# Forgetting attention: the second copy of k is taken from the first one in SBUF, and the last pair of heads is shaped one head later

## The chip, the core and the metric

One core of a Trainium2 chip runs the whole layer as one program. The metric is the device time of one execution in microseconds (us). The kernel before takes 1297.82 us, the median of three executions (1297.64 to 1299.04).

TensorE (PE) multiplies matrices and transposes; ScalarE (ACT) and VectorE (DVE) scale, copy and reduce; GpSimd (POOL) and SyncE (SP) mostly issue DMA transfers. TensorE writes its results to eight PSUM banks, everything else lies in SBUF.

## The reference, cut to what matters

The layer is a feed-forward block, a mixing block, and a second feed-forward block over 512 tokens of width 1024, in fp32. The mixing block has an mLSTM branch (4 heads) and a forgetting attention (16 heads of width 64); gates join the branches. The change touches the forgetting attention:

```python
q = jnp.moveaxis(rms_norm(q, q_g), 1, 2)
k = jnp.moveaxis(rms_norm(k, k_g), 1, 2)
logits = jnp.einsum('bhqd,bhkd->bhqk', q_blk, k).astype(f32) * scale + (F_blk[..., :, None] - F[..., None, :])
logits = jnp.where(k_pos[None, :] <= q_pos[:, None], logits, -jnp.inf)
p = jax.nn.softmax(logits, axis=-1)
return jnp.einsum('bhqk,bhkd->bhqd', p.astype(v.dtype), v)
```

## The kernel before, in words

**Two-part numbers.** To keep fp32 accuracy, an operand x is split into a rounded high part (type fp32r) and a low part, x minus high. A product takes three matmuls, high by high, high by low, low by high (`mm3`, L145 to L147). ScalarE makes the high part (`split`, L120) and VectorE the low part (L122) of every weight tile.

**The attention stage.** Heads go in pairs: pair p holds heads 2p and 2p+1, and two pairs make a group g. `fox_qkv` (L1354) multiplies the group's q and k; for groups 1 to 3 they are written to HBM (L1386) and come back turned, 16 small transfers into four tiles `fT` (`bring`, `blocks`, L1350). These lie in the tag `tok`, which has 4 buffers. For group 0, TensorE turns them into a PSUM bank instead (L1449).

`fox_t(p)` (L1428) brings a pair into shape: from the source `b` (a PSUM bank for pairs 0 and 1, an `fT` tile in SBUF for the others) it makes for each of the two heads a q tile with the high part in one half of the partitions and the low part in the other, a k tile with the high part in both halves, and a tile `klz` with k's low part in one half and zeros in the other. ScalarE writes the high parts (L1453) and k's second copy (L1455); VectorE writes the low parts (L1459). Two matmuls per block of queries then give all three products. In `fox_t`, ScalarE has 6 instructions for a pair and VectorE 4, each over 64 partitions and 512 columns; no transfer is issued.

The loop in `run` (from L1833) goes over n, the head: `fox_s(n)` gives scores and exponentials (L1483 and L1484 on TensorE, L1486 and L1490 on VectorE, L1494 on ScalarE), `fox_o(n-2)` multiplies by v (L1543, L1546, L1547), then perhaps `fox_t`, then `fox_p(n-1)` scales the rows (L1507 on ScalarE from head 9 on), transposes them into three PSUM banks (L1513) and splits these (L1511 on ScalarE, L1512 on VectorE). The scores and these transposes take turns in the four banks of the pool `pt`. Between these calls `advance(fill, ...)` steps through work that keeps TensorE busy: projections of the next group and gates (L1591), and from n = 12 on the output gate of the mLSTM branch, `y_a(m)`: it loads the weights of m+1 (`raw`, L107) and then the tile `ht` of m+1 (L1350, also in the tag `tok`), and computes `th` (L1570) and `ya` (L1572, L1573). `out_sums` forms sums of `w_out` on the side (`so`, `wo`, with POOL's queue).

**Order.** A planner at build time gives each engine one fixed order: it follows the program's order as a priority, and lets a later instruction go first where it thinks the earlier one isn't ready. Buffers of a tag are given out as they come free. On the chip each engine takes its instructions strictly in that order.

Of the kernel before, what the change touches and what calls it, by code (L numbers as in the profile page):

```python
# [14 lines left out]
AF = mybir.ActivationFunctionType  # L15
# [32 lines left out]
class Layer:  # L48
# [36 lines left out]
    def advance(self, gen, n):  # L85
        for _ in range(n):
            if next(gen, self) is not self:
                self.tick()
            for p in self.posts[:]:
                p[0] -= 1  # L90
                if p[0] < 0:
                    self.posts.remove(p)
                    p[1]()
# [1334 lines left out]
    def fox_t(self, p, ap):  # L1428


        nc = self.nc
        g, pr = p // 2, p % 2
        tok, vt = self.fx[g]
        if p < 2:

            self.klz[p] = [ap.tile([P, T], F32R, name=f"klz{p}{h}", tag="qk", bufs=16) for h in range(2)]
            for h in range(2):
                nc.gpsimd.memset(self.klz[p][h][64 - h * 64:P - h * 64, :].bitcast(F32), 0.0)
        lohi = (slice(0, 64), slice(64, P))
        new = lambda n: ap.tile([P, T], F32R, name=self.nm(n), tag="qk", bufs=16)  # L1440
        q, k, kl = [new("fq") for _ in range(2)], [new("fk") for _ in range(2)], self.klz[p % 2]
        for i, R in ((0, R_FQ), (1, R_FK)):
            if g:
                b = tok[2 * i + pr]
            else:
                b = self.tbank()
                c = i * 256 + pr * P
                for tb in range(NT):
                    nc.tensor.transpose(b[:, tb * P:(tb + 1) * P], tok[tb][:, c:c + P], self.ident)  # L1449
            gc = self.colA[:, R + p:R + p + 1]  # L1450
            for h in range(2):
                own, oth = lohi[h], lohi[1 - h]
                nc.scalar.activation((q, k)[i][h][own, :], b[own, :], AF.Copy, scale=gc[own, :])  # L1453
                if i:
                    nc.scalar.activation(k[h][oth, :], b[own, :], AF.Copy, scale=gc[own, :])  # L1455
            for h in range(2):
                own, oth = lohi[h], lohi[1 - h]
                lo = q[h][oth, :] if i == 0 else kl[h][own, :]
                nc.vector.scalar_tensor_tensor(lo, b[own, :], gc[own, :], (q, k)[i][h][own, :], op0=MUL, op1=SUB)  # L1459
        self.qkt[p] = (q, k, kl)  # L1460
# [164 lines left out]
    def run(self):  # L1625
        nc, tc, A = self.nc, self.tc, self.A
# [10 lines left out]
        with tc.tile_pool(name="f1t", bufs=1) as tp:  # L1637
# [5 lines left out]
            with tc.tile_pool(name="f1h", bufs=1) as hp:  # L1643
# [8 lines left out]
                n = 0  # L1652
# [118 lines left out]
        yp = ys.enter_context(tc.tile_pool(name="y", bufs=1))  # L1771
# [22 lines left out]
        with tc.tile_pool(name="att", bufs=1) as ip:  # L1794
            self.maskM = ip.tile([P, P], F32, name="maskM")
            self.maskF = ip.tile([P, P], F32, name="maskF")
            for t, fill, sgn in ((self.maskM, BIG, 1), (self.maskF, -BIG, -1)):

                nc.gpsimd.memset(t, 0.0)
                nc.gpsimd.affine_select(t, t, pattern=[[sgn, P]], compare_op=ALU.is_ge, fill=fill,  # L1800
                                        base=0, channel_multiplier=-sgn)
            self.onz = ip.tile([P, NT, 2], F32, name="onz")
            nc.gpsimd.memset(self.onz[:, :, 0:1], 1.0)
            nc.gpsimd.memset(self.onz[:, :, 1:2], 0.0)
            self.hom = ip.tile([P, NK], F32, name="hom")
            nc.vector.tensor_scalar(self.hom, self.colA[:, R_OM:R_OM + NK], 0.5, None, op0=MUL)
            self.hmg = ip.tile([P, NK], F32, name="hmg")
            nc.vector.tensor_scalar(self.hmg, self.colA[:, R_MG:R_MG + NK], 0.5, None, op0=MUL)
            self.hgg = yp.tile([P, 64], F32, name="hgg")[:, 0:2 * NK]
            nc.vector.tensor_scalar(self.hgg, self.colA[:, R_GG:R_GG + 2 * NK], 0.5, None, op0=MUL)  # L1810
            self.klz = [None] * 2
            self.g_next = None
            self.vt, self.W, self.fx, self.qkt, self.S = [None] * 4, {}, {}, {}, {}
            advance = self.advance
            advance(self.v_mlstm(0, ip, ip), 99)

            gates = iter([(m, i) for i in range(2) for m in range(NK)][2:])
            def with_gates(gen, n):
                yield from gen
                todo = [next(gates) for _ in range(n)]  # L1820
                for mi, then in zip(todo, todo[1:] + [None]):
                    yield from self.gate(*mi, ip, then=then)
            for h0, n, fill in ((0, 3, with_gates(self.v_mlstm(1, ip, ip), 1)), (2, 4, with_gates(self.fox_qkv(0, ip), 3))):
                for f, h in ((self.mlstm_w, h0), (self.mlstm_w, h0 + 1), (self.mlstm_h, h0), (self.mlstm_h, h0 + 1)):
                    f(h, ip)
                    for i in range(n):
                        advance(fill, 1)
                        if f == self.mlstm_w and h >= 2 and i < 2:
                            next(early)
                        if f == self.mlstm_h and h == 3 and i == 0:  # L1830
                            self.fox_t(0, yp)
                advance(fill, 99)
            for n in range(18):  # L1833
                if n % 4 == 0 and n < 16:
                    advance(fill, 99)
                    g = n // 4
                    fill = with_gates(self.fox_qkv(g + 1, ip), (2, 2, 6)[g]) if g < 3 else (s for m in range(NK) for s in self.y_a(m, yp, ip))
                last = n >= 12
                if n < 16:
                    self.fox_s(n, ip)  # L1840
                    advance(fill, 1 if last or n == 1 else 2)
                    if n == 0:
                        advance(fill, 2)
                    elif n == 1:
                        self.fox_t(1, yp)
                        advance(fill, 2)
                if n > 9:
                    next(pw, None)
                if n >= 2:
                    self.fox_o(n - 2, ip)  # L1850
                    advance(fill, 1)
                if n > 9:
                    next(pw, None)
                if n % 2 and 1 < n < 13:
                    self.fox_t((n + 1) // 2, yp)
                    if n == 11:
                        self.fox_t(7, yp)
                if 1 <= n < 17:
                    self.fox_p(n - 1, ip)
                    advance(fill, 1 if last else 2)  # L1860
                if n == 9:
                    pw = self.out_sums(A["w_out"][0], ip)
                if 9 < n < 12:
                    next(pw)
            advance(fill, 99)
            for m in range(NK):
                self.dump(f"ya_{m}", self.ya[m])
                self.dump(f"yb_{m}", self.yb[m])

        self.ntmp, self.xn_tiles, self.gb_tag = 4, self.xn_branch, ("sg", 2)  # L1870
        with tc.tile_pool(name="br", bufs=1) as bp:
# [17 lines left out]
            for m in range(NK):  # L1889
# [3 lines left out]
                if m >= NK - 2:  # L1893
                    n = ("A11", "A12")[m - NK + 2]
# [25 lines left out]
        with tc.tile_pool(name="f2t", bufs=1) as tp, tc.tile_pool(name="f2h", bufs=1) as hp:  # L1920
# [8 lines left out]
            n = 0  # L1929
# [39 lines left out]
```

## Time and profile before

| what | us |
|---|---|
| median of 3 executions (range) | 1297.82 (1297.64 to 1299.04) |
| the profiled execution, whole | 1298.22 |
| its span, first to last instruction | 1296.4 |
| TensorE busy | 1284.4 |
| VectorE busy | 984.2 |
| ScalarE busy | 657.3 |

[...] A view of the profile lists either groups of instructions, or single ones in order of time with the idle time of their engine before them and what ended it. TensorE's matmuls overlap, so its idle times are somewhat smaller than the time lost from one start to the next.

### The profile page before, as it was taken

Reading aid. Unit: us, or ns where it says so; the run is one execution under the profiler, and the core shown is the slowest. Engines: PE = TensorE matmul, PEld = TensorE weight load, DVE = VectorE, ACT = ScalarE, POOL = GpSimd, SP = SyncE. Lnnn points to the kernel's source line nnn. Section 1 sums busy time; section 2 is a strip of 40 time slices with the busy share of each in tenths; the row PEclk is TensorE's granted clock in tenths of the full one; section 3 lists DMA queues with packets and bytes.
Section 4 is the critical chain, followed back from the end, with each engine's and each line's share of the span. In section 5 each row is a group of like instructions: output and inputs, shape, how many; then the busy total and the mean of one; then the engine's idle time right before and its main releaser. Section 6 shows DMA issues by size and latency. Waiting matters only on the chain.

```text
span 1296.4 us, 17850 instructions
## 1 busy us (share of the span) xinstructions
PE 1284.4 (99%) x6244; PEld 1080.5 (83%) x6244; DVE 984.2 (76%) x1776; ACT 657.3 (51%) x1096; POOL 34.3 (3%) x73
## 2 busy tenths in 40 slices
PE   7999999999999999999999999999999999999998
PEld 6888888888899888888888888888898888888887
DVE  6888777678688778989997776778977656535787
ACT  5523323266467656666575786344683233223752
POOL 1000000000010101000001100000000000000000
PEclk9999999999999999999999999999999999999999
DMA  9989998756875634545456895876649868634584
GB/s 293 293 305 323 327 301 290 223 152 183 294 199 134 187 90 131 182 131 156 138 125 178 249 196 143 240 238 200 195 152 331 279 231 267 218 98 136 167 270 150
DMA packets 247322, 272.02 MB, mean 210 GB/s; under 512 B 57840, under 2 KB 183440, under 8 KB 247232
## 3 DMA queue, kind: packets, MB, share of 16 engines
q1 hardware_dynamic: 240096, 254.55, 64.0%
q10 hardware_dynamic: 4384, 7.88, 2.0%
q0 software_dynamic: 2752, 8.45, 2.0%
q8 instruction: 49, 0.80, 0.3%
q14 instruction: 41, 0.34, 0.1%
HBM read 227.77 MB, written 43.06 MB: 209 GB/s over the span
## 4 chain that ended last, share of the span: by engine, by line
PE 86%; DVE 5%; DMA 4%; ACT 3%; issue 1%; SPq 0%; POOL 0%; ACTq 0%; DVEq 0%; POOLq 0%
PE g L145 22%; PE g L146 22%; PE g L147 22%; PE t L146 4%; PE t L147 4%; PE t L145 4%; PE g L1124 1%; PE t L1543 1%; PE t L1124 1%; PE t L1513 1%; DMA ar<-in_w_ada_dram 1%; DMA raw<-in_ffn_w_out_dram 1%; PE t L1484 1%; PE t L1483 1%; DVE wl L122 1%
## 5 line engine op out<-in xcount | busy, mean ns | idle before, releaser
L120 ACT ACTIVATE wh<-raw 128x1024 fp32r<-128x1024 f32 (+2 forms) x245 | 240.1, 989 | 348.4 <-DMA raw<-in_ffn_w_in_dram 118.3
L122 DVE TENSOR_TENSOR wl<-raw,wh 128x1024 fp32r<-128x1024 f32 (+2 forms) x245 | 275.9, 1134 | 131.9 <-ACT wh L120 124.5
L145 PE MATMUL g<-uh,wh 128*128 128x512 f32 (+1 forms) x872 | 338.0, 388 | 0.1
L147 PE MATMUL g<-uh,wl 128*128 128x512 f32 (+1 forms) x872 | 336.5, 386 | 0.0
L146 PE MATMUL g<-ul,wh 128*128 128x512 f32 (+1 forms) x872 | 336.0, 385 | 0.0
L147 PEld LDWEIGHTS g<-uh,wl 128*128 128x128 f32 x872 | 163.8, 188 | 33.5
L145 PEld LDWEIGHTS g<-uh,wh 128*128 128x128 f32 x872 | 163.9, 188 | 32.7 <-issue 0.6
L146 PEld LDWEIGHTS g<-ul,wh 128*128 128x128 f32 x872 | 163.9, 188 | 32.2
L145 PE MATMUL g<-wh,uh 128*128 128x512 f32 (+1 forms) x256 | 97.7, 382 | 0.0
L147 PE MATMUL g<-wh,ul 128*128 128x512 f32 (+1 forms) x256 | 96.5, 377 | 0.0
L146 PE MATMUL g<-wl,uh 128*128 128x512 f32 (+1 forms) x256 | 96.4, 376 | 0.0
L328 DVE SCALAR_TENSOR_TENSOR acc<-raw,ccol,acc 128x1024 f32<-128x1024 f32 (+1 forms) x49 | 54.8, 1128 | 47.8 <-DMA raw<-in_w_ada_dram 47.8
L146 PE MATMUL t<-wl,A 128*128 128x512 f32 x176 | 68.6, 390 | 0.6 <-DVE wl L122 0.6
L145 PE MATMUL t<-wh,A 128*128 128x512 f32 x176 | 68.4, 390 | 0.0
L147 PEld LDWEIGHTS g<-wh,ul 128*128 128x128 f32 x256 | 48.2, 188 | 9.0
L146 PEld LDWEIGHTS g<-wl,uh 128*128 128x128 f32 x256 | 48.3, 188 | 8.3
L145 PEld LDWEIGHTS g<-wh,uh 128*128 128x128 f32 x256 | 48.2, 188 | 8.3
L145 PE MATMUL g<-yh,wh 128*128 128x512 f32 x128 | 49.9, 390 | 0.0
L147 PE MATMUL g<-yh,wl 128*128 128x512 f32 x128 | 49.8, 389 | 0.0
L146 PE MATMUL g<-yl,wh 128*128 128x512 f32 x128 | 49.8, 389 | 0.0
L1494 ACT ACTIVATE S<-S,mn 128x128 f32<-128x128 f32 (+1 forms) x64 | 35.6, 557 | 25.2 <-DVE mn L1486 13.9
L466 ACT ACTIVATE A<-E 128x768 fp32r<-128x768 f32 x22 | 18.6, 845 | 48.9 <-DVE E L465 48.9
(412 smaller groups left out, 2299.7 us busy)
## 6 DMA issues: line engine op xcount, KB each, us to landing
raw<-in_ffn_w_in_dram SPq DMA_DIRECT2D x79, 512.0 KB
raw<-in_w_ada_dram SPq DMA_DIRECT2D x48, 512.0 KB
raw<-in_w_mix_dram SPq DMA_DIRECT2D x46, 512.0 KB
sa<-in_ffn_w_out_dram SPq DMA_DIRECT2D x22, 512.0 KB
ws<-sa SPq DMA_DIRECT2D x22, 512.0 KB
raw<-ws SPq DMA_DIRECT2D x44, 256.0 KB
raw<-in_ffn_w_out_dram SPq DMA_DIRECT2D x22, 512.0 KB
sb<-in_ffn_w_out_dram SPq DMA_DIRECT2D x43, 256.0 KB
```

The costliest lines, as they stand in the source:

```text
L120: nc.scalar.activation(hi[:, c], src[:, c], AF.Copy)
L122: self.last_lo = nc.vector.tensor_tensor(lo[:, c], src[:, c], hi[:, c], op=SUB)
L145: pin(mm(ps, lh, rh, start=start, stop=False, skip_group_check=on))
L146: pin(mm(ps, lh, rl, start=False, stop=False, skip_group_check=on))
L147: self.last_mm = pin(mm(ps, ll, rh, start=False, stop=stop, skip_group_check=on))
L328: nc.vector.scalar_tensor_tensor(a, r[:, s], c, a, op0=MUL, op1=ADD)
L466: nc.scalar.activation(A1[:, 0:3, :], E[:, 0:3, :], AF.Copy)
L1124: pin(nc.tensor.matmul(acc_ps[b], ws[m][p == 1][:, c:c + P], self.ul[m] if p == 2 else self.uh[m], start=m == 0 and p == 0, stop=m == NK - ...
L1483: nc.tensor.matmul(ps[:, :w], q[:, s], k[:, :w], start=True, stop=False)
L1484: nc.tensor.matmul(ps[:, :w], q[:, s], kl[:, :w], start=False, stop=True)
L1494: nc.scalar.activation(S[:, ws], S[:, ws], AF.Exp, scale=-1.0, bias=m, accum_out=sm[:, qb:qb + 1])
L1513: tr = lambda b, c, qb, kb: nc.tensor.transpose(b[:, c:c + P], S[:, P_OFF[qb] + kb * P:P_OFF[qb] + (kb + 1) * P], self.ident)
```

## The change

In `fox_t`, the second copy of k's high part (L1455) no longer reads the source `b` with a scale per partition. It is a plain copy of the first one, already rounded, from the other half of the partitions in SBUF. It stands in the second loop, after both first copies and ahead of the low part.

In the loop of `run`, `fox_t(7)` moves from n = 11, where it stood right behind `fox_t(6)`, to n = 12, behind `fox_o(10)` and the step of `y_a` after it. The other pairs stay where they were.

```diff
             for h in range(2):
                 own, oth = lohi[h], lohi[1 - h]
                 nc.scalar.activation((q, k)[i][h][own, :], b[own, :], AF.Copy, scale=gc[own, :])
-                if i:
-                    nc.scalar.activation(k[h][oth, :], b[own, :], AF.Copy, scale=gc[own, :])
             for h in range(2):
                 own, oth = lohi[h], lohi[1 - h]
+                if i:
+                    nc.scalar.activation(k[h][oth, :], k[h][own, :], AF.Copy)
                 lo = q[h][oth, :] if i == 0 else kl[h][own, :]
                 nc.vector.scalar_tensor_tensor(lo, b[own, :], gc[own, :], (q, k)[i][h][own, :], op0=MUL, op1=SUB)
...
-                if n % 2 and 1 < n < 13:
-                    self.fox_t((n + 1) // 2, yp)
-                    if n == 11:
-                        self.fox_t(7, yp)
+                if n % 2 and 1 < n < 13 or n == 12:
+                    self.fox_t(n // 2 + 1, yp)
```

## Rows read from the trace of the kernel before

**Rows 1.** The page, part 1: busy us, share of the span, instructions of an engine.
```profile
PE 1284.4 (99%) x6244; PEld 1080.5 (83%) x6244; DVE 984.2 (76%) x1776; ACT 657.3 (51%) x1096; POOL 34.3 (3%) x73
```

**Rows 2.** Waits of TensorE, whole span: line, awaited; us in total, times, longest.
```profile
PE t L216 <- DMA rowsC<-in_b_ada_dram: 5.1, 1, 5.1
...
PE t L1483 <- DVE Pl L1512: 0.7, 1, 0.7
...
PE t L1484 <- DVE klz L1459: 0.5, 1, 0.5
```

**Rows 3.** Stretches of 15 us: length, then each engine's busy us, clock, DMA share.
```profile
735.00:750.00 15.00, 15.00 (x77) 12.67 (x77) 10.61 (x28) 14.67 (x30) 1.42 (x3) 1.00 0.71 213
750.00:765.00 15.00, 14.16 (x75) 11.66 (x74) 10.61 (x29) 12.74 (x29) 0.93 (x2) 1.00 1.05 194
765.00:780.00 15.00, 15.00 (x79) 12.77 (x78) 11.17 (x31) 11.54 (x27) 2.32 (x5) 1.00 0.85 210
```

**Rows 4.** Order of time, TensorE: start, us, instruction; head 12's first and last scores.
```profile
754.06 0.22 PE L1483 MATMUL t<-fk,fq 128*128 128x128 f32 x1
...
756.36 0.39 PE L1484 MATMUL t<-klz,fq 128*128 128x512 f32 x1
```

**Rows 5.** Order of time, TensorE: the scores of heads 13 and 14.
```profile
767.65 0.22 PE L1483 MATMUL t<-fk,fq 128*128 128x128 f32 x1
...
768.69 0.39 PE L1484 MATMUL t<-klz,fq 128*128 128x512 f32 x1
...
779.56 0.22 PE L1483 MATMUL t<-fk,fq 128*128 128x128 f32 x1
```

**Rows 6.** Order of time, TensorE, scores of head 0; in brackets idle before, releaser.
```profile
549.85 0.65 PE L1484 MATMUL t<-klz,fq 128*128 128x128 f32 x3 [0.46 <-DVE klz L1459]
550.64 0.47 PE L1483 MATMUL t<-fk,fq 128*128 128x512 f32 x1
```

**Rows 7.** Order of time, VectorE: k's low parts of pair 0 and of pair 1.
```profile
548.96 1.53 DVE L1459 SCALAR_TENSOR_TENSOR klz<-t,colA,fk 64x512 fp32r<-64x512 f32 x2
...
568.25 1.51 DVE L1459 SCALAR_TENSOR_TENSOR klz<-t,colA,fk 64x512 fp32r<-64x512 f32 x2 [1.12 <-ACT fk L1455]
```

**Rows 8.** Order of time, ScalarE, pair 0: the last of four k copies.
```profile
548.21 0.69 ACT L1455 ACTIVATE fk<-t,colA 64x512 fp32r<-64x512 f32 x1
```

**Rows 9.** Groups by shape, ScalarE: busy us, mean ns of one, idle before.
```profile
L1455 ACT ACTIVATE fk<-fT,colA 64x512 fp32r<-64x512 f32 x12 | 8.7, 722 | 0.3
...
L1455 ACT ACTIVATE fk<-t,colA 64x512 fp32r<-64x512 f32 x4 | 2.7, 684 | 0.1
...
L372 ACT ACTIVATE hl<-yb 64x512 fp32r<-64x512 f32 x2 | 1.2, 624 | 0.0
```

**Rows 10.** Order of time, ScalarE: pair 7's first and last instruction; th; Ph.
```profile
739.37 0.71 ACT L1453 ACTIVATE fq<-fT,colA 64x512 fp32r<-64x512 f32 x1
...
747.78 0.72 ACT L1455 ACTIVATE fk<-fT,colA 64x512 fp32r<-64x512 f32 x1
...
752.40 0.69 ACT L1570 ACTIVATE th<-g,hom 128x512 f32<-128x512 f32 x1
...
753.60 1.35 ACT L1511 ACTIVATE Ph<-t 128x512 fp32r<-128x512 f32 x3
```

**Rows 11.** Order of time, ScalarE: Ph of head 11, then y_a's weights.
```profile
764.45 1.36 ACT L1511 ACTIVATE Ph<-t 128x512 fp32r<-128x512 f32 x3 [0.62 <-PE t L1513]
...
766.30 1.16 ACT L120 ACTIVATE wh<-raw 128x512 fp32r<-128x512 f32 x2
```

**Rows 12.** Waits between 735 and 775 us, weight loads of TensorE.
```profile
PEld g L145 <- ACT wh L120: 0.2, 1, 0.2
```

**Rows 13.** Order of time, SP's queue: loads for y_a.
```profile
749.35 4.38 SPq L1350 DMA_DIRECT2D ht<-h_d  x4
753.77 0.50 SPq L107 DMA_DIRECT2D raw<-in_w_mix_dram  x1
```

**Rows 14.** DMA issues from 560 to 900 us: KB each, median us to landing.
```profile
so<-in_w_out_dram POOLq DMA_DIRECT2D x8, 512.0 KB, 5.2
```

## The prediction, made before the changed kernel was run

> **What bounds the kernel now.** I read the page's busy times first. TensorE is busy for 1284.4 of 1296.4 us at the full clock [rows 1], so at most 12 us of the span are not TensorE's own work, and the change neither adds nor removes a matmul. What it can give is a part of TensorE's idle time, and what it can cost is new idle time. The waits of TensorE come next [rows 2]: the longest, 5.1 us, is for the first load at the start of the kernel and out of reach. Two of the others lie in the attention: 0.7 us for `Pl` (the split transposes) and 0.5 us for `klz`, which `fox_t` makes. The stretches of 15 us show where the first belongs: between 735 and 750 us ScalarE is busy for 14.67 of 15 us, and TensorE then loses 0.84 us in the stretch behind it, at head 12 [rows 3]. ScalarE, with half of the span busy, is thus the bound for a few microseconds around the last pairs, and nowhere else here.
>
> An idle time understates a loss, because matmuls overlap. Head 12's eight score matmuls take 756.36 - 754.06 = 2.30 us from the first start to the last [rows 4], head 13's the same eight 768.69 - 767.65 = 1.04 us [rows 5]. So the stall at head 12 costs 1.26 us, where about 0.8 us of idle time is shown: a factor of 1.6, which I use below as an estimate.
>
> **The second copy of k, pairs 0 and 1.** In pair 0, TensorE waits 0.46 us for `klz`, and the fourth score matmul starts 550.64 - 549.85 - 0.65 = 0.14 us after the third has ended [rows 6]. Together 0.60 us idle, or about 0.9 us lost by the factor above. Why `klz` is late: its two instructions start at 548.96 [rows 7], right at the end, 548.21 + 0.69 = 548.90, of ScalarE's fourth read of the same bank [rows 8]. Pair 1 says the same without a doubt: there VectorE sat idle for 1.12 us until ScalarE's last `fk` copy from the bank [rows 7]. With the change only the two first copies read the bank. The last copy, which the planner had put behind other work, and one copy of 0.68 us before it are no longer in front of `klz`. Pair 1's low parts can start 2 x 0.684 = 1.37 us earlier [rows 9], and pair 0's by up to 3 us, of which TensorE needs less than one. So I take away the whole 0.9 us; the bounds are 0 and 0.9. What is next in line is the second copy of head 0 itself, which now comes third on ScalarE and not second, one instruction of 0.68 us later; the score matmuls that read it had TensorE busy with gate matmuls ahead of them, so I put this at nothing, and at up to 0.7 us if that cover is gone.
>
> [...]
>
> **The price of the copy itself.** From `fT` in SBUF with a scale per partition it takes 722 ns, from the bank 684 ns. A plain copy of the same shape from SBUF to the rounded type takes 624 ns [rows 9]. So 12 x 98 + 4 x 60 ns = 1.4 us of ScalarE's time go, out of reach of the path except for the four copies of pairs 6 and 7, 0.4 us, which lie in the full stretch. Both copies that the change swaps move by one instruction; for pairs 1 to 7 many microseconds lie between `fox_t` and the scores, so this costs nothing.
>
> [...]
>
> **`fox_t(7)` one head later.** Before, its six instructions on ScalarE lie from 739.37 to 748.50 [rows 10], in the full stretch [rows 3]. They take 2 x 0.72 + 2 x 0.72 + 2 x 0.62 = 4.1 us, and VectorE's four some 4 x 0.76 = 3.0 us, by the length of `klz` [rows 7]. Behind them wait, in ScalarE's order, the exponentials of head 11, the scalings, `th` and then `Ph` of head 10 at 753.60 [rows 10], from which `Pl` is made, which frees the bank for which head 12's scores wait [rows 2]. Of these 4.1 us, more than the 1.26 us of the stall, all or none leaves this chain, as the planner decides. If they leave, the stall goes whole. They then compete with heads 12 and 13: ScalarE is idle for 15 - 12.74 = 2.3 us from 750 to 765 and for 15 - 11.54 = 3.5 us from 765 to 780 [rows 3], 5.7 us against 4.1 us. In the first stretch alone they don't fit, 1.8 us would be pushed out; `Ph` of head 11 has 0.62 us of idle time ahead of it [rows 11] and the rest may reach head 13. So the new loss is between 0 and 1.2 us. I take 0.45, a third of the old stall, since the work that is relieved ahead moves up as well. Pair 7 itself is not late: it ended at 748.50 and head 14 starts at 779.56 [rows 5], and a head lasts 767.65 - 754.06 = 13.6 us.
>
> No transfer is issued in `fox_t(7)`, so POOL's queue has nothing of it; the `so` sums of `out_sums` on VectorE, for which POOL waits, only come nearer the front. SP's queue is different: it waits for buffers that `fox_t(7)` gives back, which is the slower rival below.
>
> **Sum.** Profiled execution 1298.22 - 0.9 (head 0) - 1.26 (head 12) + 0.45 (new loss) = 1296.5 us, all with the same 1.8 us outside the span. The median of the three runs lies 0.4 us under the profiled execution, so I predict 1296.1 us. A third small wait, 0.2 us for `y_a`'s weights behind a crowded ScalarE [rows 12], some 0.3 us with the factor, is left as it is.
>
> **The rivals.**
>
> - *All three stalls go and none comes* (for it: 5.7 us of room; against: the room is not where it is needed first). 0.9 + 1.26 + 0.3 = 2.5 us less: 1295.3.
> - *The move does nothing.* The planner lets later work go ahead: `th` at 752.40, which belongs to n = 12, already stands in front of `Ph` of head 10, which belongs to n = 11 [rows 10]. It may pull `fox_t(7)` forward in the same way, to where it was. Then 0.9 us remain: 1296.9.
> - *Head 0 gains nothing*, since its own second copy comes later or the planner leaves `klz` behind the same work: -0.8 us alone, 1297.0.
> - *Slower, by SP's queue.* The four `tok` buffers of the last group go to `ht`: pair 6's two to ht(0) and ht(1), pair 7's to ht(2) and ht(3). SP issues ht(2) at 749.35 and behind it the weights `raw` at 753.77 [rows 13]; these are split at 766.30 [rows 11]. Of the 766.30 - 753.77 = 12.5 us, a transfer of this size takes some 5.2 us [rows 14], so 7.3 us are to spare. If pair 7's q tile is read only after 749.35 + 7.3 = 756.7 us, all of SP's queue, then ScalarE's, then TensorE is late by every further microsecond. If `fox_t(7)` went behind `fox_o(10)`, as the program has it, its q would be done about 762: 5.3 us lost, less 2.2 gained, 1300.9. For it speaks the program's order; against it, the planner gives ht(2) a place only where it thinks a buffer free and can let `raw` pass.
>
> **How the numbers follow.** Chances: forecast 0.46, all stalls gone 0.16, the move does nothing 0.17, head 0 gains nothing 0.07, slower 0.14. A measurement of this kernel can tell about 0.2%, 2.6 us, from no change: that is below 1295.2 or above 1300.4. The first needs the ceiling of 2.5 us and a little more, which the factor of 1.6 leaves open: 0.14. The second needs most of the slower rival: 0.09. Within 0.2%: 0.77. The range takes the ceiling less 0.5 us for the scatter of medians, 1294.8, and on the upper side no gain at all with a small SP delay, 1298.9; some 0.1 is left out above and 0.1 below.
>
> **What would show it.** Right: pair 0's `klz` no longer starts at the end of the last `fk` copy and TensorE's `klz` wait is gone; the `fk` copies take about 0.62 us; ScalarE is busy for 11 to 12 of 15 us from 735 to 750; head 12's scores take 1.04 us. Wrong: `fox_t(7)` still before 750 us; a new wait of TensorE for `wh`, `Pl` or `Ph` between 755 and 775 us; idle time in front of ScalarE's `ya` or `wh` that ends with a DMA, with ht(2) issued after 757 us. A difference of the times without a difference in these waits would mean that my picture of a TensorE that is bound everywhere else is wrong.

## The result, and the profile after

| | median us | range | executions |
|---|---|---|---|
| before | 1297.52 | 1296.12 to 1300.00 | 12 |
| after | 1300.36 | 1298.71 to 1302.13 | 12 |

The ratio is 1.0019, 95% interval 1.0011 to 1.0028: slower by 1.4 to 3.6 us where 1.4 us less had been forecast, and above the predicted range. The profiled execution of after took 1298.71 us with a span of 1296.9 us, that of before 1298.22 us, both at a granted TensorE clock of 1.000. These two differ by 0.5 us only; why they understate the loss stands in the last section. Three executions of 2157 to 3341 us, two of e12 and one of before beside e13 to e16, are left out of every median here.

**A correction to the prediction, needed to read on.** Its head numbers are one too low. Each head has four score matmuls of L1483; the one at 754.06 us [rows 4] is the 53rd of the 64, so it belongs to head 13 and not 12. Likewise `Ph` at 753.60 [rows 10] is that of head 11, that of [rows 11] is that of head 12, and rows 5 show heads 14 and 15. So pair 7, which is heads 14 and 15, is needed at 767.65 and not at 779.56 us; in after its last instruction ends at 756.3, in time even so. From here on the numbers are the right ones, except in the quoted expectations of e1 to e4: their `Ph` of head 10 is that of head 11, and their stall at head 12 is that of head 13.

The page and the waits of TensorE, whole span, after (us in total, times, longest), answering [rows 1, 2]:

```profile
PE 1285.2 (99%) x6244; PEld 1080.7 (83%) x6244; DVE 983.7 (76%) x1776; ACT 656.0 (51%) x1096; POOL 34.4 (3%) x73
```

```profile
PE t L216 <- DMA rowsC<-in_b_ada_dram: 5.5, 1, 5.5
PE t L1483 <- DVE Pl L1512: 0.9, 1, 0.9
PE t L1483 <- DVE yb L1547: 0.6, 1, 0.6
PE t L1005 <- DMA ar<-in_w_ada_dram: 0.5, 1, 0.5
PE t L1483 <- DVE mn L1490: 0.3, 1, 0.3
PE g L145 <- ACT wh L120: 0.3, 1, 0.3
```

The wait for `klz` is gone, as forecast. The wait for `Pl`, which was to vanish, is longer (0.9 us, before 0.7), and three waits inside the attention are new: for `mn`, for `yb` and for `wh`. They are those of the scores of head 1, of the scores of head 4, and of the output gate `y_a` behind head 13's scores, in order of time on TensorE, after:

```profile
559.33 0.47 PE L1483 MATMUL t<-fk,fq 128*128 128x512 f32 x1 [0.27 <-DVE mn L1490]
...
603.95 0.33 PE L1483 MATMUL t<-fk,fq 128*128 128x128 f32 x1 [0.58 <-DVE yb L1547]
...
762.18 0.50 PE L145 MATMUL g<-uh,wh 128*128 128x512 f32 x1 [0.26 <-ACT wh L120]
```

Since idle times understate losses (with `Pl` at head 13, after, 0.87 us of idle time go with 1.13 us lost against e15), I also compare stretches: the time from the start of one matmul of TensorE to that of another, the 6244 matmuls numbered by start. In before, number 2550 starts at 527.77 us, 2700 at 558.45, 2850 at 582.52, 3000 at 608.68, 3450 at 699.46 and 3800 at 770.30; a few matmuls change places inside a stretch. The names are those of the texts quoted below: the scores of heads 1 and 2 fall into the second stretch, those of heads 3 and 4 into the third, those of heads 10 to 14 into the last.

| us | head 0: 2550 to 2700 | head 1: 2700 to 2850 | heads 2 to 4: 2850 to 3000 | around head 13: 3450 to 3800 |
|---|---|---|---|---|
| before | 30.68 | 24.07 | 26.17 | 70.85 |
| before, another execution (e5) | 30.52 | 24.07 | 26.18 | 70.27 |
| after | 29.93 | 24.57 | 27.46 | 70.83 |
| after, another execution (e3) | 29.82 | 24.68 | 27.43 | 70.88 |

The stretches between 3000 and 3450 and from 3800 to the last matmul differ by less than 0.1 us between the four; those ahead of 2550 scatter from one execution to the next. So there is one gain, about 0.7 us at head 0; two losses where the prediction had nothing, about 0.55 us at head 1 and 1.27 us in heads 2 to 4; and around head 13, where 0.8 us net were to be gained, nothing against one execution of before and 0.6 us of loss against the other.

**The loss at heads 1 to 4 begins on VectorE at head 0.** In order of time on VectorE, before, and then after; the bracket gives the idle time before an instruction:

```profile
546.27 0.17 DVE L172 SCALAR_TENSOR_TENSOR rq<-rt,rq 128x4 f32<-128x4 f32 x1
547.41 1.51 DVE L1342 STREAM_TRANSPOSE hn<-hn 128x512 f32<-128x512 f32 x2 [0.97 <-ACT hn L1339]
548.96 1.53 DVE L1459 SCALAR_TENSOR_TENSOR klz<-t,colA,fk 64x512 fp32r<-64x512 f32 x2
550.72 0.69 DVE L1475 TENSOR_TENSOR Am<-A,maskF 128x512 f32<-128x512 f32 x1 [0.23 <-DMA h_d<-hn]
551.56 0.29 DVE L1486 CUSTOM_DVE_ANT_0 S<-t,Am 128x128 f32<-128x128 f32 x1
```

```profile
544.91 0.74 DVE L1459 SCALAR_TENSOR_TENSOR klz<-t,colA,fk 64x512 fp32r<-64x512 f32 x1
...
545.76 0.76 DVE L1459 SCALAR_TENSOR_TENSOR klz<-t,colA,fk 64x512 fp32r<-64x512 f32 x1
...
547.14 0.16 DVE L172 SCALAR_TENSOR_TENSOR rq<-rt,rq 128x4 f32<-128x4 f32 x1
548.28 1.51 DVE L1342 STREAM_TRANSPOSE hn<-hn 128x512 f32<-128x512 f32 x2 [0.98 <-ACT hn L1339]
554.04 0.69 DVE L1475 TENSOR_TENSOR Am<-A,maskF 128x512 f32<-128x512 f32 x1 [4.24 <-DMA h_d<-hn]
...
555.90 0.29 DVE L1486 CUSTOM_DVE_ANT_0 S<-t,Am 128x128 f32<-128x128 f32 x1
```

`klz` of pair 0, free of the bank earlier, now goes ahead of the small operations that end in `rq`, the scale of the mLSTM branch's last `hn`. Then VectorE sits idle for 4.24 us ahead of `Am`. The trace names the transfer that ended nearest, `h_d`; but `Am` reads `A`, a row of decay factors that `fox_s` loads over ScalarE's queue. In order of time on ScalarE and its queue (ACTq), before and then after:

```profile
546.47 0.51 ACT L1339 ACTIVATE hn<-hn,rq 128x256 f32<-128x256 f32 x1 [0.42 <-DVE rq L172]
546.49 0.33 ACTq L1468 DMA_DIRECT2D A<-A_d  x1
...
550.00 0.46 ACTq L1468 DMA_DIRECT2D A<-A_d  x1
```

```profile
547.34 0.51 ACT L1339 ACTIVATE hn<-hn,rq 128x256 f32<-128x256 f32 x1 [0.54 <-DVE rq L172]
547.41 0.33 ACTq L1593 DMA_DIRECT2D g_d<-tg  x1
...
547.77 0.44 ACTq L1468 DMA_DIRECT2D A<-A_d  x1
...
548.26 0.47 ACTq L1468 DMA_DIRECT2D A<-A_d  x1
```

Counted from matmul 2550, `rq` starts 1.39 us later (546.27 - 527.77 = 18.50, then 547.14 - 527.25 = 19.89), ScalarE's scaling of `hn` with it, and the load of `A` behind that 1.80 us later. It now also goes out between a store of 256 KB (`g_d`) and head 1's load, and is used 6.3 us after its issue, not 4.2. So head 0's reductions start 4.9 us later (28.65 and not 23.79 us behind matmul 2550). VectorE makes up most of that before 563 us: the last reduction of head 1 starts 35.74 us behind matmul 2550, in before 34.84, so 0.9 us late. For the rest there is no room behind it. Stretches of 15 us (length, then PE, PEld, DVE, ACT, POOL busy, clock, DMA share and GB/s), before:

```profile
570.00:585.00 15.00, 15.00 (x112) 14.30 (x111) 14.96 (x42) 8.40 (x18) 0.00 (x0) 1.00 0.35 104
585.00:600.00 15.00, 15.00 (x86) 13.16 (x85) 14.90 (x42) 9.99 (x22) 0.00 (x0) 1.00 0.65 158
```

From 570 to 600 us VectorE is busy for 29.86 of 30 us, beside a TensorE that is just as full. What it is late by when it enters, it can hardly make up before head 4; e14 and e17 below put a number to that.

**The loss at head 13.** ScalarE in order of time, after:

```profile
750.83 0.69 ACT L1570 ACTIVATE th<-g,hom 128x512 f32<-128x512 f32 x1 [1.58 <-PE g L147]
751.42 0.71 ACT L1572 ACTIVATE ya<-ht,hmg 128x512 f32<-128x512 f32 x1
752.03 1.45 ACT L1453 ACTIVATE fq<-fT,colA 64x512 fp32r<-64x512 f32 x2
753.51 1.47 ACT L1453 ACTIVATE fk<-fT,colA 64x512 fp32r<-64x512 f32 x2
755.00 1.29 ACT L1457 ACTIVATE fk<-fk 64x512 fp32r<-64x512 f32 x2
756.20 1.32 ACT L1511 ACTIVATE Ph<-t 128x512 fp32r<-128x512 f32 x3
```

Pair 7's six instructions stand right ahead of `Ph` of head 11, from which `Pl` is made, for which head 13's scores wait; and a little further ahead, in front of `th`, ScalarE idles for 1.58 us. `Ph` starts at 756.20, in before at 753.60 [rows 10]. The stretches of 15 us, answering [rows 3]:

```profile
735.00:750.00 15.00, 15.00 (x78) 12.75 (x77) 8.32 (x24) 12.36 (x27) 0.89 (x2) 1.00 0.85 222
750.00:765.00 15.00, 13.87 (x75) 11.32 (x74) 11.31 (x29) 12.89 (x27) 0.00 (x0) 1.00 0.82 158
765.00:780.00 15.00, 15.00 (x77) 12.75 (x76) 12.39 (x32) 12.89 (x30) 3.01 (x6) 1.00 0.96 224
```

ScalarE was relieved from 14.67 to 12.36 us in the first stretch, and yet TensorE idles for 1.13 us in the second (0.87 for `Pl` and 0.26 for `wh`), 0.84 before. The first of the head's scores and the one that waits (answering [rows 4]):

```profile
754.47 0.22 PE L1483 MATMUL t<-fk,fq 128*128 128x128 f32 x1
...
757.55 0.39 PE L1483 MATMUL t<-fk,fq 128*128 128x256 f32 x1 [0.87 <-DVE Pl L1512]
```

### The profile page after: what moved, and what is told of

Read it like the earlier page. It is cut to its first block, busy times and chain, and to the rows that moved or that the text cites. A ratio compares the mean times of both kernels' runs of the same rounds, so it can differ in the third digit from the quotient of the medians.

```text
span 1296.9 us, 17847 instructions
## 1 busy us (share of the span) xinstructions
PE 1285.2 (99%) x6244; PEld 1080.7 (83%) x6244; DVE 983.7 (76%) x1776; ACT 656.0 (51%) x1096; POOL 34.4 (3%) x73
## 4 chain that ended last, share of the span: by engine, by line
PE 86%; DVE 7%; DMA 3%; ACT 2%; issue 1%; SPq 0%; POOL 0%; ACTq 0%; DVEq 0%; POOLq 0%
PE g L147 22%; PE g L146 22%; PE g L145 22%; PE t L145 4%; PE t L146 4%; PE t L147 4%; PE g L1124 1%; PE t L1543 1%; DVE wl L122 1%; PE t L1124 1%; PE t L1513 1%; DMA ar<-in_w_ada_dram 1%; DMA h_d<-hn 1%; PE t L1483 1%; PE t L1484 1%
```

## The experiments

The theories, as the quoted texts name them: A, the loss is the move, by the pile ahead of `Ph`; B, it is the copy, by the order in heads 0 to 4; C, it is elsewhere. Of head 13's stall in before: D, it belongs to that execution; E, to the program. Of head 4: F, the order of TensorE's matmuls there; G, pairs 0 and 1. Later: P and S for the place and the source of the copy, L for `A`'s late load, K for the low parts themselves. A2, in the text of e8, is A by the right count. e1 to e4 ran beside the same executions of before (median 1296.86 us), as did e5 to e8 (1296.43), e9 to e12 (1297.07) and e13 to e16 (1297.01); e17 stands beside 1297.19. The ratio is not formed from these two medians, so the two can differ by some 0.0004. The stretches, from one profiled execution each:

| us | median us | ratio to before, 95% | head 0 | head 1 | heads 2 to 4 | around head 13 |
|---|---|---|---|---|---|---|
| e1 copy alone | 1297.71 | 1.0008 (1.0000 to 1.0017) | 30.02 | 24.43 | 27.46 | 69.49 |
| e2 move alone | 1297.61 | 1.0002 (0.9993 to 1.0011) | 30.68 | 24.07 | 26.18 | 70.79 |
| e3 after again | 1298.73 | 1.0018 (1.0009 to 1.0027) | 29.82 | 24.68 | 27.43 | 70.88 |
| e4 after, pair 7 at n = 13 | 1298.28 | 1.0013 (1.0004 to 1.0022) | 30.05 | 24.63 | 27.48 | 70.09 |
| e5 before again | - | - | 30.52 | 24.07 | 26.18 | 70.27 |
| e6 copy, pair 2 | - | - | 30.54 | 24.07 | 26.45 | 69.66 |
| e7 copy, other fill at head 4 | 1297.26 | 1.0005 (0.9996 to 1.0014) | 30.04 | 24.77 | 26.83 | 69.49 |
| e8 after, pair 7 behind `fox_p(11)` | 1298.81 | 1.0018 (1.0008 to 1.0028) | 29.89 | 24.61 | 27.48 | 70.18 |
| e9 source only | 1297.08 | 1.0004 (0.9995 to 1.0013) | 30.53 | 24.07 | 26.64 | 69.45 |
| e10 place only | - | - | 30.43 | 24.06 | 26.48 | 70.27 |
| e11 copy, pairs 0 and 1 | - | - | 29.98 | 24.58 | 27.73 | 69.49 |
| e12 copy, pairs 6 and 7 | 1296.86 | 0.9998 (0.9989 to 1.0007) | 30.57 | 24.07 | 26.21 | 70.73 |
| e13 copy, `A` early | 1296.51 | 0.9997 (0.9988 to 1.0005) | 29.86 | 24.07 | 26.64 | 69.44 |
| e14 copy, pair 0 | - | - | 29.88 | 24.23 | 27.22 | 69.75 |
| e15 copy, pair 1 | - | - | 30.53 | 24.06 | 26.63 | 69.47 |
| e16 before, `A` early | 1296.83 | 1.0002 (0.9991 to 1.0012) | 30.55 | 24.06 | 26.16 | 69.63 |
| e17 copy, pair 0, `A` early | 1297.09 | 1.0000 (0.9990 to 1.0009) | 29.80 | 24.07 | 26.23 | 69.60 |

**e1 to e4: the two parts apart, after again, and the move one head further.** e1 has the diff's hunk in `fox_t` alone, e2 its hunk in `run` alone, e3 is after. e4 is after with

```diff
-                if n % 2 and 1 < n < 13 or n == 12:
+                if n % 2 and 1 < n < 12 or n == 13:
                     self.fox_t(n // 2 + 1, yp)
```

> The copy alone: k's second copy from SBUF, pair 7 stays at n = 11. Theory A (the loss comes from the move: pair 7's six ScalarE instructions now stand as one block ahead of Ph of head 10, and what is behind them has less room for late transfers): this kernel is 0 to 0.9 us faster than before, about 1297.0 where before is 1297.5, and it shows the new small stalls at heads 1 and 3 and none of klz. Rival B (the loss comes from the copy, through the order that the planner makes of it at heads 0 to 3): this kernel is 2 to 3 us slower than before, about 1300.

> The move alone: pair 7 shaped at n = 12, k's second copy as before. Theory A: slower than before by 2 to 3.5 us, about 1300.3, with the same wide scatter of the executions as the changed kernel, and the klz wait at head 0 still there. Rival B: within 0.7 us of before.

> The changed kernel, profiled once more, to see an execution other than the first one, which was among the fastest of its twelve (1298.71 against a median of 1300.36). Theory A: if this execution is slower than the first, the extra time stands between 745 and 775 us, as a wait of ScalarE or TensorE that ends with a transfer or with Ph. Rival C (nothing in the attention: transfers elsewhere, as at the start or in the feed-forward blocks): the extra idle time of TensorE stands elsewhere.

> Both parts, but pair 7 is shaped at n = 13, one head later still: its six ScalarE instructions then stand behind Ph of head 10 and partly behind head 12's exponentials. Theory A: the 1.1 us stall at head 12 is gone and the time is 1.5 to 3 us under the changed kernel's, about 1297.5 to 1298.5. Rival B: no change against the changed kernel, about 1300.3. If later is simply worse (SP's queue waits for pair 7's buffers), slower still by 1 us or more.

Neither A nor B holds alone. The copy has the gain at head 0 and the losses at heads 1 to 4 and no loss at head 13; the move has after's long stretch around head 13 and is as before elsewhere. The medians are 0.85 us (copy), 0.75 us (move) and 1.87 us (both) above before; the ratios say 1.0, 0.3 and 2.3 us, with intervals from 0 or below for each part alone. So the totals show a loss for both parts together only, and what each part does is read from the stretches. One head later (e4) 0.74 us of the stretch around head 13 come back, and 0.45 us of the median, where theory A expected 1.5 to 3.

**e5 to e8.** e5 is before again; e6 has the copy's edit for pair 2 only (`if i and not (p == 2)` at the old place, `if i and (p == 2)` at the new one); e7 is e1 with one step of other work ahead of head 4's scores; e8 is after with pair 7 behind `fox_p(11)`:

```diff
-                    self.fox_s(n, ip)
-                    advance(fill, 1 if last or n == 1 else 2)
+                    advance(fill, int(n == 4)); self.fox_s(n, ip)
+                    advance(fill, 1 if last or n in (1, 4) else 2)
```

```diff
-                if n % 2 and 1 < n < 13 or n == 12:
+                if n % 2 and 1 < n < 12:
                     self.fox_t(n // 2 + 1, yp)
                 if 1 <= n < 17:
-                    self.fox_p(n - 1, ip)
+                    self.fox_p(n - 1, ip); n == 12 and self.fox_t(7, yp)
```

> The kernel before, profiled once more. Theory D: the stall of 1.26 us at the scores that start at 754 us (head 13's, by a count of the score matmuls) belongs to the one profiled execution, in which the tile fT of pair 6 landed late: ScalarE's first fq of pair 6 started 18.26 us behind the 3500th matmul of TensorE, against 16.40 to 17.48 in four of the other traces. In another execution, with fq at 17.5 or earlier, head 13's eight scores take 1.04 to 1.3 us and not 2.30. Rival E: the stall belongs to the program; the scores take 2.2 to 2.4 us again wherever fq lies.

> Only pair 2's second copy of k is taken from the first; all other pairs and the place of pair 7 as before. On TensorE this changes the planned order at head 4 alone, where the score matmuls come 1 to 4 projection matmuls earlier. Theory F (the 1.3 us lost at head 4 come from that order): the stretch from the 2850th to the 3000th matmul takes 27.4 us instead of 26.2, head 0 has its klz wait as before. Rival G (they come from pairs 0 and 1, through the work that these push back): 26.2 us.

> The copy alone, and at n = 4 the first step of the next projection is put ahead of head 4's scores in the program, so that TensorE has 12 matmuls of it before them. Theory F: the stretch from the 2850th to the 3000th matmul falls back to 26.2 to 26.4 us, head 0 keeps its gain of 0.7 us, and the time is 0.9 to 1.4 us under that of the copy alone, at or up to 0.5 us under that of the kernel before. Rival G: the stretch stays at 27.4 us.

> The changed kernel with fox_t(7) at n = 12 behind fox_p(11) and not ahead of it. On ScalarE this puts pair 7's six instructions behind Ph of head 11, for which head 13's scores wait. Theory A2 (the stall at head 13 comes from these six standing ahead of Ph): Ph of head 11 starts 2.5 to 4 us earlier than in the changed kernel, head 13's eight scores take 1.04 us instead of 4.47 (with some projection matmuls between), and the stretch from the 3700th to the 3950th matmul is 0.6 to 1.4 us shorter than the changed kernel's 49.25. Rival: the pile moves on and head 14 or 15 loses the same.

*Head 13's stall in before: nearer to D.* In e5 head 13's eight scores take 1.84 us, neither E's 2.2 to 2.4 nor D's 1.04 to 1.3, and `fq` came at 17.68 us, later than D had asked for. ScalarE waits for pair 6's `fT`, and its whole queue behind it, `Ph` of head 11 last, shifts with the landing, in the same order in both executions of before (722 to 757 us). First `fq` of pair 6 and that `Ph`, in order of time on ScalarE, of before (whose `Ph` is in [rows 10]), of e5 and of e1:

```profile
727.40 0.72 ACT L1453 ACTIVATE fq<-fT,colA 64x512 fp32r<-64x512 f32 x1 [3.54 <-DMA fT<-t_d]
```

```profile
726.38 0.72 ACT L1453 ACTIVATE fq<-fT,colA 64x512 fp32r<-64x512 f32 x1 [2.67 <-DMA fT<-t_d]
...
752.58 1.34 ACT L1511 ACTIVATE Ph<-t 128x512 fp32r<-128x512 f32 x3
```

```profile
725.25 0.72 ACT L1453 ACTIVATE fq<-fT,colA 64x512 fp32r<-64x512 f32 x1 [1.77 <-DMA fT<-t_d]
...
751.53 1.34 ACT L1511 ACTIVATE Ph<-t 128x512 fp32r<-128x512 f32 x3
```

The first and the last of head 13's scores in e1, in order of time on TensorE:

```profile
753.66 0.22 PE L1483 MATMUL t<-fk,fq 128*128 128x128 f32 x1
...
754.70 0.39 PE L1484 MATMUL t<-klz,fq 128*128 128x512 f32 x1
```

`Ph` starts 26.20, 26.20 and 26.28 us behind `fq`. Against the head's first score matmul it starts 0.46 us ahead in before, 2.13 us ahead in e1, where the eight scores take 754.70 - 753.66 = 1.04 us: no stall. Over the fourteen profiled executions here that leave pair 7 at n = 11, the stretch around head 13 runs from 69.44 to 70.85 us, mean 69.83, and its two longest, 70.85 and 70.73 (before and e12), are those whose `fq` came latest behind matmul 3500, 18.26 and 18.09 us; at 17.67 and 17.68 us it is 70.27; where it came before 16.9 us, the stretch is 69.44 to 69.49. In e12 the time is lost one head earlier, by the same wait (TensorE, in order of time), and head 13's scores take 1.04 us:

```profile
743.91 0.50 PE L1483 MATMUL t<-fk,fq 128*128 128x512 f32 x1 [0.62 <-DVE Pl L1512]
```

In the three with the move at n = 12 it is 70.79 to 70.88, whether `fq` came at 16.64 or at 17.20 us. Against e15, which has no stall (69.47), after loses 1.13 us between matmul 3725 and 3750, where `Pl` is awaited, and 0.25 us between 3750 and 3775, where `wh` is. The move thus turned a stall of 0 to 1.4 us that hung on a landing into one of 1.4 us that was there in all three: 70.83 - 69.83 = 1.0 us lost on the mean of the fourteen. That mean is over several kernels. Before's own two executions have 70.85 and 70.27, and against their mean the move costs 0.3 us; whether before's landings are late by chance or by its order is not shown.

*The pile, taken away (e8).* `Ph` goes first, head 13's scores have no stall, and the next user of ScalarE waits. ScalarE, then TensorE, in order of time:

```profile
752.06 1.34 ACT L1511 ACTIVATE Ph<-t 128x512 fp32r<-128x512 f32 x3
753.28 1.46 ACT L1453 ACTIVATE fq<-fT,colA 64x512 fp32r<-64x512 f32 x2
...
760.00 0.61 ACT L120 ACTIVATE wh<-raw 128x512 fp32r<-128x512 f32 x1
```

```profile
760.67 0.50 PE L145 MATMUL g<-uh,wh 128*128 128x512 f32 x1 [0.75 <-ACT wh L120]
```

TensorE now waits for `y_a`'s weights, which ScalarE splits behind pair 7. Of the 1.4 us, 0.65 come back in the stretch; the total (1.0018) is no better than that of after.

*Head 4.* With pair 2's edit alone (e6) TensorE's order at head 4 is, but for the place of one matmul, the one of after, and the stretch loses 0.28 us of 1.28: F falls as the main cause. More work ahead of head 4's scores (e7) covers 0.63 us of it, while head 1 is 0.34 us longer there than in e1.

**e9 to e12: source or place, and which pairs.** e9 takes the plain copy from `k` but leaves it in the first loop; e10 puts the copy into the second loop but takes it from `b` with its scale:

```diff
-                    nc.scalar.activation(k[h][oth, :], b[own, :], AF.Copy, scale=gc[own, :])
+                    nc.scalar.activation(k[h][oth, :], k[h][own, :], AF.Copy)
```

```diff
                 nc.scalar.activation((q, k)[i][h][own, :], b[own, :], AF.Copy, scale=gc[own, :])
+            for h in range(2):
+                own, oth = lohi[h], lohi[1 - h]
                 if i:
                     nc.scalar.activation(k[h][oth, :], b[own, :], AF.Copy, scale=gc[own, :])
-            for h in range(2):
-                own, oth = lohi[h], lohi[1 - h]
                 lo = q[h][oth, :] if i == 0 else kl[h][own, :]
```

e11 and e12 have the whole edit of the copy under `p < 2` and `p >= 6`.

> Half of the copy's part: k's second copy is made from the first in SBUF, but it stays where it was, each right behind its own first copy, ahead of the low parts; pair 7 at n = 11 as before. It tells apart which half of the edit costs something behind head 0. Stretches of TensorE between the same numbered matmuls; before has 30.5 to 30.7 us at head 0 (matmuls 2550 to 2700), 24.07 us at head 1 (2700 to 2850) and 26.17 us at heads 2 to 4 (2850 to 3000); with the whole edit of the copy they are 30.0, 24.5 and 27.46. Theory P (the place: the second copies stand behind both first ones and come later in the engine's queue): head 0 about 30.0, since the bank is read only twice, heads 1 to 4 as before, 24.07 and 26.2; the time is then 0.6 us below before, ratio 0.9995. Theory S (the source: VectorE's low parts start earlier once the bank is read only twice, and what they displace is late): 30.0, then 24.5 and 27.4, and the time about 0.9 us above before.

> The other half: the second copies of k stand behind both first ones, as in the change, but are still made from the bank (or from fT) with their scale; pair 7 at n = 11. Theory P: head 1 about 24.5 and heads 2 to 4 about 27.4 us, as with the whole edit. Theory S: 24.07 and 26.2, as before. At head 0 both expect no gain or little, 30.3 to 30.7 us, since the bank is read four times by ScalarE as before. This is one look, so its total is not compared, only the stretches.

> The copy's edit for pairs 0 and 1 alone (those that read the bank); pairs 2 to 7 and the place of pair 7 as before. With the edit for pair 2 alone, the stretch of heads 2 to 4 cost 0.28 us more than before, with the edit in all pairs 1.28. Theory G (the rest is pairs 0 and 1: their work comes earlier and pushes that of the next projection back): head 0 about 30.0, head 1 24.5, heads 2 to 4 27.2 to 27.5 us. Theory F (it is the order of TensorE's matmuls at head 4 that goes with pair 2): head 0 about 30.0, head 1 24.1 to 24.5, heads 2 to 4 26.2 us.

> The copy's edit for pairs 6 and 7 alone; the order of TensorE's instructions is that of before, and heads 0 to 4 are untouched. It takes 4 x 0.1 = 0.4 us off ScalarE's chain ahead of the exponentials of head 11. If the copy's shorter duration is worth anything where ScalarE is full, head 13's scores (matmuls 3700 to 3800) take 0 to 0.4 us less than 20.1 to 20.55 us, as the landing of pair 6's fT falls; all other stretches as before. Time 1296.0 to 1296.9 against 1296.4 to 1296.9 of before, ratio 0.9997 to 1. A loss of over 0.5 us would mean that the edit costs something at the last pairs too.

Neither half makes the whole loss, and neither makes the gain: P and S both fall as stated. Only with both together does the planner put `klz` ahead of the chain of `rq`: in e9 and in e10 it starts 0.19 us behind the start of `rq`, in after 2.2 us ahead of it. `Am` waits 4.3 us in e11, 1.7 in e9 and 1.8 in e10. Pairs 0 and 1 alone (e11) have all of it: G. The shorter copies of pairs 6 and 7 (e12) bring nothing: its `fT` was late, and the stretch is as long as `fq`'s landing makes it.

**e13 to e17: `A`'s late load taken away.** e13 is e1, e16 is before and e17 is the copy's edit under `p == 0`, each with

```diff
+            self.A0 = ip.tile([P, T], F32, name="A00")
+            nc.scalar.dma_start(self.A0, self.A_d[0:1, :].to_broadcast([P, T]))
             for h0, n, fill in ((0, 3,
...
-        A0 = self.A0 if h else bring(0)
+        A0 = self.A0
```

e14 and e15 have the copy's edit under `p == 0` and `p == 1`, with `A` as before.

> The copy's edit in all pairs (pair 7 at n = 11, as before), and head 0's row of A, which fox_s(0) loads itself, is loaded ahead of the matrix-memory heads, into a tile of its own. With the edit, klz of pair 0 goes on VectorE ahead of the chain that ends in rq; ScalarE's scaling of hn, which waits for rq, comes 1.4 us later, and the load of A that is issued behind it 1.8 us later, together with g_d's store and A's second load; Am (what head 0's scores are reduced with) starts 26.8 us behind TensorE's matmul 2550 and not 23.0. Theory L (this late load is what costs heads 1 to 4): Am no longer waits for a transfer; head 0 stays at 30.0 us, head 1 goes back to about 24.1 and heads 2 to 4 to 26.2 to 26.5, and the time is 0.3 to 0.7 us below before (ratio 0.9995 to 0.9998). Theory K (the low parts of pairs 0 and 1, which go earlier, push VectorE's other work back, whatever A does): 24.5 and 27.4 as with the edit alone, time 0.9 us above before.

> The copy's edit for pair 0 alone. Theory L (A's late load, which comes with klz of pair 0): head 0 30.0 us, head 1 24.5, heads 2 to 4 26.9 to 27.7 us, nearly all of what pairs 0 and 1 together cost; Am again about 26.8 us behind matmul 2550. Theory K for pair 1's low parts: head 1 24.07 and heads 2 to 4 26.2 us.

> The copy's edit for pair 1 alone. Theory L: head 0 30.6, head 1 24.07, heads 2 to 4 26.2 to 26.5 us (the order of VectorE around pair 2 changes as with pair 2 alone, which cost 0.28 us), Am about 23 us behind matmul 2550. Theory K for pair 1: 24.5 and about 27.2 us.

> Before with head 0's row of A loaded ahead of the matrix-memory heads, nothing else: a control for the early load. In before Am waits only 0.23 us for a transfer, so both theories expect all stretches within 0.1 us of before (30.5 to 30.7, 24.07, 26.2) and a time equal to that of before, ratio 1.0000 within 0.0005. Less than that would mean that the early load has a gain of its own, which then has to be taken off what the run beside it shows.

> The copy's edit for pair 0 alone, with head 0's row of A loaded ahead of the matrix-memory heads; pairs 1 to 7 and the place of pair 7 as before. Theory L: head 0 keeps its gain, 29.9 us against 30.5 to 30.7; heads 1 and 2 to 4 are those of before, 24.07 and 26.2 us, since neither A is late nor pairs 1 and 2 reordered. Net 0.6 to 0.7 us below before, ratio 0.9995, which is within what a measurement of this kernel can tell from no change: 1295.9 to 1296.6 us. If head 1 or heads 2 to 4 are over 0.3 us longer than before, klz's new place on VectorE costs something beside A.

`Am` in e13 and in e14, VectorE in order of time:

```profile
550.02 0.65 DVE L1475 TENSOR_TENSOR Am<-A,maskF 128x512 f32<-128x512 f32 x1
```

```profile
553.34 0.69 DVE L1475 TENSOR_TENSOR Am<-A,maskF 128x512 f32<-128x512 f32 x1 [3.88 <-DMA h_d<-hn]
```

With `A` early, `Am` waits for nothing, head 0 keeps its 0.7 us, head 1's loss is gone, and of the 1.28 us at heads 2 to 4, 0.46 are left (e13). Just as much is lost by pair 1's edit alone (e15), in which `A` is on time. Pair 0's edit alone loses 0.16 + 1.04 us and holds `Am` back for 3.9 us (e14); with `A` early it loses 0.06 us (e17). The control (e16) has the stretches of before. That shows `A`'s late load as the cause of 1.2 us, theory L, and leaves 0.46 us to pair 1. The two kernels with pair 0's edit also show what becomes of the delay on VectorE: counted from matmul 2550, the last reduction of head 0 starts at 30.90 us in e14 and at 25.79 in e17, that of head 1 at 35.33 and 33.96, that of head 2 at 53.22 and 51.89. Of 5.1 us, 1.4 are left before the full stretch, and 1.3 are still there in it. How much of `A`'s delay is the later issue and how much the slower transfer was not taken apart. In e15 the planner puts, on VectorE, the first `fq` of pair 2 ahead of reductions that stood before it, and on TensorE some of head 4's scores a few matmuls earlier or later; that this is what costs the 0.46 us wasn't tried by itself.

In its stretches e17 is 0.7 us shorter than before at head 0 and equal up to head 4, but in the total neither it (1.0000) nor e13 (0.9997) can be told from before. No kernel here is shown to beat before.

## Why the prediction was wrong, point by point

- **Head 0: right in size, by more than the bank alone.** 0.9 us were taken, with bounds of 0 and 0.9; the stretch gives 0.7. `klz` starts at 544.91, 0.14 us behind the end of ScalarE's last read of the bank at 544.77, and no longer behind a fourth [rows 7, 8]. ScalarE in order of time, after:

```profile
544.09 0.68 ACT L1453 ACTIVATE fk<-t,colA 64x512 fp32r<-64x512 f32 x1
```

In both executions `klz` starts behind ScalarE's last read of the bank: 548.96 behind 548.90 us in before, 544.91 behind 544.77 in after; and pair 1's 1.12 us in before [rows 7] end with such a read. But in before pair 0's `klz` stood right behind `hn`'s transposes on VectorE as well, which end at 547.41 + 1.51 = 548.92 us. In e9 it goes ahead of them and behind `rq`, and head 0 gains nothing; the gain came only where the planner put it ahead of the chain of `rq` too.
- **"For pairs 1 to 7 ... this costs nothing", and pair 0 "by up to 3 us, of which TensorE needs less than one": the step that failed for the copy.** It priced the two copies that swap places and what `klz` gains, but not what `klz`, going 3.5 us earlier, pushes back on VectorE: 1.39 us for `rq`, then ScalarE's `hn`, then, in that queue, a load. The cost was 0.55 + 1.27 us where nothing was put, over twice the gain. For `fox_t(7)` the prediction did name who waits behind it on its engine; for `klz` it did not.
- **"ScalarE ... is thus the bound for a few microseconds around the last pairs, and nowhere else here": no run speaks against it, but it looks at ScalarE alone.** VectorE, at 76% of the span, is full from 570 to 600 us, and the prediction has no term for it.
- **The head count: the step that failed for the move.** With the numbers one too low, `fox_t(7)` at n = 12 seemed to come behind the `Ph` that mattered ("they then compete with heads 12 and 13"). By the right count `fox_p(11)`, whose `Ph` frees head 13's bank, is what the program calls right behind `fox_t(7)`: the 4.1 us, which were to leave that chain, stayed in it and now stand at its end. The relief from 735 to 750 us came, a little smaller than forecast (12.36, against 11 to 12), and did not reach `Ph`, which starts 2.6 us later. One of the prediction's own signs of being wrong came with it: new waits of TensorE between 755 and 775 us, for `Pl` at 757.55 and for `wh` at 762.18.
- **The 1.26 us stall: not a fixed size.** It was that of one execution. A second execution of before has 0.80 us (1.84 - 1.04), and the mean over the fourteen executions is 69.83 - 69.44 = 0.4 us. "If they leave, the stall goes whole" could thus have brought 0.4 to 1.0 us on the mean, and not 1.26; the move cost 0.3 to 1.0.
- **The copy's price: right in size, with no gain to be seen from it (e12).** 0.63 us for 0.68 and 0.72; ScalarE is busy for 656.0 us, 1.3 less, where 1.4 was forecast. Pair 0's copies, which read the bank in before and SBUF in after, became 0.05 us shorter, but they also lost their scale operand; what the source alone is worth there is not shown.
- **The rivals.** All stalls go, head 0 gains nothing, the move does nothing: none came. The slower rival had a chance of 0.14 and, with 1300.9 us, a time near the measured one; that is luck, since its mechanism did not come. ht(2) went out at 752.15 and not 749.35 [rows 13], and the weights behind it at 754.10 instead of 753.77; pair 7's q was read from 752.03, before the 756.7 us from which that rival decides, and no wait for `raw` or `ht` follows.

Sum, with the mean of the fourteen at head 13: -0.7 (head 0) + 0.55 + 1.27 (heads 1 to 4) + 1.0 (head 13) = +2.1 us, and +1.4 us with before's own two executions there; measured, 0.0019 x 1297.5 = 2.5 us, interval 1.4 to 3.6.

## What to carry to other kernels

An instruction that becomes ready earlier is also a delay for whatever the planner had ahead of it (here `klz`, 3.5 us earlier, puts `rq` 1.39 us back): follow the displaced chain through the engines, above all to transfers issued from a compute engine's queue, and look whether the engine that would have to make it up has any idle time in the stretch that follows. Place a moved block against the instruction that the critical wait names, by counting instances from the start. A stall seen in one profiled execution may be a late transfer of that execution (head 13's was 1.26 us in one of before and 0.80 us in the other); before it is booked as a gain, see whether it is there in a second one.

## What the runs showed of the hardware that was not expected

- The landing of pair 6's `fT`, 16 small transfers each, moved by 2.5 us over the kernels here (15.79 to 18.26 us behind matmul 3500), and between two executions of the same kernel by 0.6 us (before 18.26 and 17.68) and 0.5 us (after 17.20 and 16.67); on ScalarE a chain of 26.2 to 26.6 us behind it moved with it in the fourteen executions.
- The stretch from matmul 1000 to 1600, untouched by any of these kernels, took 137.71 us in before's profiled execution, where TensorE waits 0.57 us for `wl` at 334.82, 137.10 us in after's, and 136.60 to 137.57 us in the seventeen others. That, and before's long stretch around head 13, hid the loss between the two profiled executions.
- A load of 256 KB was used 4.2 us after its issue in before, where nothing else left ScalarE's queue within 1.8 us of it, and 6.3 us after in after, where it went out between a store and another load of its size. That these neighbours are the cause is not shown.
- A plain ScalarE copy of 64x512 took 0.63 us, the copy with a scale per partition from the same memory 0.72. Instructions that write `fk`, after (shortest, median and longest in ns):

```profile
L1457 ACT ACTIVATE fk<-fk x16: 617/631/633, 544.8 to 755.7; 64x512 fp32r<-64x512 f32 x16
L1453 ACT ACTIVATE fk<-fT,colA x12: 708/718/723, 600.1 to 754.3; 64x512 fp32r<-64x512 f32 x12
```
